# Hybrid RWKV-7 / retention trunk on one core: order of loads, small matrix visits and solves inside the scans, and one visit for four norm sums

## The chip, the cores and the metric

One core of a Trainium2 chip runs the whole program. The metric is the device time of one launch in microseconds (us). PE is the tensor engine, DVE the vector engine, ACT the scalar engine, POOL the GpSimd engine, SP the engine that issues the DMAs. Each of them works through its own instructions in program order; semaphores make one wait for another.

## What is computed

Two layers over 256 latent and 256 context tokens, width 2048. The change lies wholly in the first one, whose core is a delta-rule scan over a 64x64 state of each of 32 heads, in two directions:

```python
def wkv7_scan(S0, r, decay, k, v, kk, a, reverse):
    def step(S, inp):
        r_t, w_t, k_t, v_t, kk_t, a_t = inp
        sa = jnp.einsum('bhvk,bhk->bhv', S, kk_t)
        S = S * w_t[:, :, None, :] - sa[..., None] * (kk_t * a_t)[:, :, None, :] + v_t[..., None] * k_t[:, :, None, :]
        return S, jnp.einsum('bhvk,bhk->bhv', S, r_t)
...
def rwkv7_mixer(h_lat, h_ctx, need_ctx, ...):
    ...
    for d in range(2):
        S_c, oc = wkv7_scan(S0, r_c, w_c[d], k_c[d], v_c, kk_c, a_c[d], d == 1)
        _, ol = wkv7_scan(S_c, r_l, w_l[d], k_l[d], v_l, kk_l, a_l[d], d == 1)
```

Afterwards come a group norm, a gate, the output product with `rk_w_out` (2048x2048), the residual, an RMS norm over the 2048 channels (the four norm sums of the title) and the second layer, which the change leaves alone.

## The kernel before

Each direction is cut into chunks of 64 tokens, eight of them (four of context, then four of latents). The 32 heads stand in pairs: `e` is one of 16 tiles of two heads, and two tiles `E` and `E + 1` are scanned at the same time as two chains. A step `s` (0 to 7) of a chain handles one chunk of both directions. On the engines it is this loop:

- `z` (L1333, PE): the chunk's rows times the state; `zc` (L1338, DVE) adds a part `zv` that needs no state.
- `u` (L1352, PE): multiplies by the inverse of a triangular 64x64 matrix, `tt`; `uc` (L1358, ACT, two instructions) puts it into `uv` with its sign turned.
- `sm` (L1365, PE): the chunk's contribution to the state; `sc` (L1378, or L1380 at s = 0; DVE, four instructions) makes the new state, which the chain's next `z` needs. `qs` (L1343, ACT) scales the old state ahead of it.

Two steps of both chains make a group `q` (0 to 3), so that a pair of tiles has four groups and the scans have 8 x 4 = 32. Each group also has four small visits of PE that work on its matrices and not on the states:

- `first` (L1290): 32 products of 32x32 (fp32 ones count as two instructions in the trace: x32), that need the loaded matrix `it` of both tiles and the small inverse `t1`; `cp1` (L1297, ACT) copies the result.
- `second` (L1303): again 32x32, makes the off-diagonal quarter of the inverse, and `cp2` (L1313, ACT, four copies of 32x128) puts it into `tt`. From then on the group's `u` may run.
- `zv` (L1278): 64x64 products of `it` and `uv`; `zvc` (L1283, ACT) copies it.
- `outs` (L1406, L1414, L1421): the group's outputs, 128x64.

All other PE work in the same stretch is large 128x128x512 matmuls: the tail of the projections (L783) at the beginning, and from L1546 on the output product `rk_w_out`, called out_chunk, whose sums DVE adds into the residual (L1555) once a PSUM bank is complete. DVE also runs `inverse` (L1113, L1120), an elimination of 60 small instructions a pair, and the group norm of finished tiles.

The order on PE, DVE, ACT and POOL is written by hand: `Wheel.at(t, ...)` gives each piece a time on a planned line, `Wheel.run` emits them in the order of these times (a piece waits where a ring of buffers that it names in `need` is full), and chains the instructions so that nothing reorders them. The times are no clock: each engine runs as soon as what it needs is there. Within a group, `h0` is the planned start, `Ts` the planned length of one chain's step (chain `E + 1` stands one `Ts` behind `E`; a chain's own step comes each 2 Ts). The numbers that the change touches are these: `UB = 0.5`, `SB = 1.05` (when `u` and `sm` of a step are due, in Ts), `first` at h0 - 1.1 Ts, `zv` at h0 - 0.7 Ts, `second` at h0 - 0.3 Ts, `outs` at h0 + 4.05 Ts.

SP is not chained by the line: its DMAs are placed by the scheduler, and it issues them in order. Of a group it issues for each of the two tiles `ft` (L1220, 896 KB: `it`, `bt` and a part of `kr` in one; L1221, 128 KB: the rest of `kr`) and two halves of `uv` (L1226, 64 KB each), and for both together `tt` (L1259, eight pieces of 16 KB). There are four `ft` buffers, two of which a group takes, so a group's loads wait for the `outs` of the group two before it.

After the scans four sums of squares a column group (`nrm`, L1574, four column groups `eg`) are put on PE one by one, each into its own 32 rows of one PSUM bank.

## Time and profile before

| | us |
|---|---|
| median of 3 runs | 2784.47 |
| lowest, highest | 2777.64, 2790.91 |
| the profiled execution, its own time | 2789.24 |
| its span, first to last instruction | 2787.4 |
| the scans, from the first `first` to the last `outs` | 1014 to 1680 |
| out_chunk on PE | 1215 to 1729 |
| norm sums (L1574) on PE | 1708 to 1735 |

The span is 1.8 us shorter than the execution's own time. In the profile's rows a group of instructions has its busy time; "idle before" is the time in which its engine had nothing running ahead of it, with the engine or the DMA that ended this. PEld is the weight load of PE, which runs beside its matmuls. PEclk is the granted clock of PE, 1.00 being full speed. In a timeline row stand the start, the length, the engine, the line, the operation, and behind an x how many instructions were merged; since the ends of matmuls are modelled and overlap, the distance between two starts tells more than a length.

### The profile page before, as it was taken

The numbers are of one execution on the slowest core, as the hardware profiler recorded it, in microseconds if no ns is written. First come the engines' busy times: TensorE is split into PE (matmuls) and PEld (weight loads), VectorE is DVE, ScalarE is ACT, GpSimd is POOL, SyncE is SP. The second block draws the span as 40 slices with busy tenths as digits, with TensorE's granted clock in tenths as the row PEclk, the third lists the DMA queues.
The fourth block names the chain that finished last, engine by engine and source line by source line (L and its number), as shares of the span: only waits on it lengthen the run. The fifth ranks groups of instructions, "written<-read, shape, count | busy, mean of one in ns | idle before, by whom it ended". The sixth has DMA issues, their size and how long they took to land. (4 is left out here: it accounts for less than half of the span.)

```text
span 2787.4 us, 48089 instructions
## 1 busy us (share of the span) xinstructions
PE 2653.6 (95%) x18580; PEld 2135.4 (77%) x18580; DVE 1704.2 (61%) x3110; ACT 1317.7 (47%) x2274; POOL 494.5 (18%) x362
## 2 busy tenths in 40 slices
PE   7999999999998999978889999999999999999998
PEld 5576478777776778867777775788888898899886
DVE  3565853678888945677667655965555643434444
ACT  5243742477777524544444443554444533334443
POOL 0002400000004232221222222210000089700000
PEclk9999999999999999998999999999999999999999
DMA  9869873569898776766657565565555666644654
GB/s 340 298 242 313 295 268 121 153 201 275 260 271 254 225 215 191 200 225 198 211 176 213 163 184 196 187 204 187 170 178 175 232 239 218 215 136 152 205 185 162
DMA packets 525686, 594.68 MB, mean 213 GB/s; under 512 B 116993, under 2 KB 358545, under 8 KB 522641
## 3 DMA queue, kind: packets, MB, share of 16 engines
q1 hardware_dynamic: 525458, 591.61, 66.6%
q8 instruction: 146, 2.39, 0.4%
q14 instruction: 82, 0.67, 0.1%
HBM read 464.11 MB, written 127.40 MB: 212 GB/s over the span
## 5 line engine op out<-in xcount | busy, mean ns | idle before, releaser
L397 DVE TENSOR_TENSOR wlo<-wraw,whi 128x1024 fp32r<-128x1024 f32 (+1 forms) x368 | 460.6, 1253 | 570.4 <-ACT whi L396 558.4
L396 ACT CAST whi<-wraw 128x1024 fp32r<-128x1024 f32 (+1 forms) x368 | 375.7, 1024 | 601.9 <-PE ps_acc L423 175.3
L423 PE MATMUL ps_acc<-whi,xop 128*128 128x512 f32 x1024 | 305.0, 392 | 1.3 <-DVE ev L645 0.8
L1919 PE MATMUL ps_acc<-xop,whi 128*128 128x256 f32 (+1 forms) x1024 | 255.8, 343 | 3.6 <-ACT whi L396 2.3
L423 PEld LDWEIGHTS ps_acc<-whi,xop 128*128 128x128 f32 x1024 | 192.1, 188 | 45.3 <-issue 2.9
L1546 PE MATMUL ps_b<-yx,whi 128*128 128x512 f32 x512 | 213.2, 445 | 5.1 <-DVE x L1555 3.6
L1919 PEld LDWEIGHTS ps_acc<-xop,whi 128*128 128x128 f32 x1024 | 178.1, 192 | 27.0 <-ACT whi L396 2.7
L1819 PEld LDWEIGHTS ps_b<-ax,xop 128*128 128x128 f32 x1536 | 190.8, 188 | 4.9 <-DVE ah L397 0.3
L1819 PE MATMUL ps_b<-ax,xop 128*128 128x256 f32 x1536 | 194.4, 282 | 0.1
L423 PE MATMUL ps_acc<-wlo,xop 128*128 128x512 f32 x512 | 187.1, 392 | 0.0
L729 PE MATMUL ps_acc<-xop,whi 128*128 128x512 f32 x512 | 177.9, 407 | 2.0 <-DVE ev L645 2.0
L580 PE MATMUL ps_acc<-xop,whi 128*128 128x512 f32 x512 | 161.7, 402 | 14.3 <-ACT xop L396 12.6
L1919 PE MATMUL ps_acc<-xop,wlo 128*128 128x256 f32 (+1 forms) x512 | 172.3, 338 | 0.0
L1358 ACT ACTIVATE uv<-ps_p 64x128 f32<-64x128 f32 x256 | 69.5, 271 | 212.1 <-PE ps_p L1352 205.8
L1869 PE MATMUL ps_acc<-whi,ah 128*128 128x512 f32 x512 | 161.6, 396 | 1.9 <-DVE ah L397 1.8
L423 PE MATMUL ps_c<-whi,xop 128*128 128x512 f32 x512 | 155.3, 390 | 0.0
L1892 POOL TENSOR_TENSOR wga<-wga,cst 128x512 f32<-128x512 f32 x64 | 71.0, 1129 | 413.1 <-DMA wga<-in_ada_w 412.9
L1537 POOL TENSOR_TENSOR wlo<-wraw,whi 128x512 fp32r<-128x512 f32 (+1 forms) x48 | 80.6, 1679 | 327.2 <-ACT whi L1536 234.4
L580 PEld LDWEIGHTS ps_acc<-xop,whi 128*128 128x128 f32 x512 | 96.1, 191 | 53.6 <-ACT xop L396 16.3
L1378 DVE SCALAR_TENSOR_TENSOR s<-ps_p,ec,qs 64x64 f32<-64x64 f32 x384 | 108.6, 283 | 28.3 <-PE ps_p L1365 21.0
L1546 PEld LDWEIGHTS ps_b<-yx,whi 128*128 128x128 f32 x512 | 97.3, 193 | 29.3 <-issue 10.5
L1113 DVE TENSOR_TENSOR invT<-invX 128x30 f32<-128x30 f32 (+14 forms) x240 | 102.0, 425 | 21.3 <-DMA invX<-Ld 15.7
(299 smaller groups left out, 5609.8 us busy)
## 6 DMA issues: line engine op xcount, KB each, us to landing
wada<-in_ada_w SPq DMA_DIRECT2D x72, 1024.0 KB, 7.8
wraw<-in_rt_w_in SPq DMA_DIRECT2D x64, 1024.0 KB, 5.2
ft<-fD SPq DMA_DIRECT2D x64, 896.0 KB, 6.9
wraw<-in_rk_w_in SPq DMA_DIRECT2D x72, 512.0 KB, 4.8
fD<-it SPq DMA_DIRECT2D x64, 512.0 KB, 4.3
wraw<-in_rt_w_in SPq DMA_DIRECT2D x64, 512.0 KB, 4.8
wraw<-in_rt_w_out SPq DMA_DIRECT2D x32, 1024.0 KB, 5.1
wraw<-in_rk_w_in SPq DMA_DIRECT2D x28, 1024.0 KB, 6.0
```

The lines of the kernel that those rows point to most:

```text
L396: self.nc.scalar.copy(hi, src)
L397: (eng or self.nc.vector).tensor_tensor(lo, src, hi.bitcast(F32), ALU.subtract)
L423: nc.tensor.matmul(pt, xop(d)[:, x_, xs], ws[k // 2][w_][:, k % 2, sl], start=(d == 0 and n == 0), stop=(d == nk - 1 and n == 2))
L580: nc.tensor.matmul(acc[i], (hi, lo)[w_][:, kk, 128 * i:128 * i + 128], xs[ds[k]][:, x_, :], start=(k == 0 and n == 0), stop=(k == nk - 1 a ...
L729: nc.tensor.matmul(st["acc"][i], st["s", d // 4][w_][:, d % 4, 128 * i:128 * i + 128], self.kx[d][:, x_, :], start=(d == 0 and m == 0), st ...
L1113: nc.vector.tensor_tensor(tmp[:, 0:j, 0:n], X[:, 0:j, j].unsqueeze(2).broadcast_to([128, j, n]), X[:, j, j + 1:].unsqueeze(1).broadcast_to ...
L1378: nc.vector.scalar_tensor_tensor(dst, src, ec, R["qs", d][H, H], ALU.mult, ALU.add)
L1537: nc.gpsimd.tensor_tensor(lo[:, 0:n, :], src, hi[:, 0:n, :].bitcast(F32), ALU.subtract)
L1546: nc.tensor.matmul(Q["p", i], Q["s", i // 2][w_][:, k, 128 * (i % 2):128 * (i % 2) + 128], st["yx", e0 + k][:, x_, :], start=(k == 0 and r ...
L1819: nc.tensor.matmul(pt[:, TL * j:TL * j + TL], ht[e][:, w_, 128 * k:128 * k + 128], ax[:, k, x_, :], start=(k == 0 and n == 0), stop=(k == ...
L1869: nc.tensor.matmul(acc[m], y[:, x_, kk, 128 * m:128 * m + 128], ws[w_][:, kk, :], start=(p == 0 and kk == 0 and n == 0), stop=(p == 7 and ...
L1919: nc.tensor.matmul(acc[i][:, 0:nt], w_[:, kk, 128 * i:128 * i + 128], x[:, x_, 0:nt], start=(d == 0 and n == 0), stop=(d == KD - 1 and n = ...
```

## The change

Five things are changed.

1. `ready` of the wheel: a piece may now ask for several buffers of one ring, so one piece `loads(E, q)` can take the `ft` buffers of both tiles.
2. The loads of both tiles are one piece, and each `ft` is loaded in three DMAs: the columns of `it` (512 KB) of both tiles, then the `uv` halves, then the rest (384 KB and 128 KB) of both.
3. `first` and `zv` stand behind each other at h0 - 0.9 Ts; `second` stands at h0 + 0.049 Ts, `outs` at h0 + 4.17 Ts, which is 0.17 Ts into the next group.
4. `u` is due at 0.62 Ts (`UB`) and `sm` at 1.15 Ts (`SB`). The columns of `first` and `second` in PSUM are those of `slot`, so `cp2` takes two copies of 32x256 instead of four of 32x128.
5. The four sums of a column group are put on PE in one piece.

The diff, without the lines that only rename:

```diff
     def ready(self, e):
+        k = {}
         for r, n, _ in e[4]:
             h = self.ring.setdefault(r, [])
-            if len(h) >= n and h[-n] not in self.gone:
+            m = n - k.get(r, 0)
+            if len(h) >= m and h[-m] not in self.gone:
                 return False
+            k[r] = k.get(r, 0) + 1
         return True
...
-UB, SB = 0.5, 1.05
+UB, SB = 0.62, 1.15
...
-            def loads(e, q):
+            def loads(E, q):
...
-                    ft = self.next_ft()
-                    nc.sync.dma_start(ft[:, :, 0:896], self.fD[e, n, :, :, 0:896])
-                    nc.sync.dma_start(ft[:, :, 960:1088], self.fD[e, n, :, :, 896:])
...
-                    w = self.sp.tile([128, 2, 2, 128], F32, name="uv", tag="uv", bufs=FR)
-                    for p in range(2):
-                        r = slice(64 * p, 64 * p + 64)
-                        nc.sync.dma_start(w[r, :, p, :], self.vcD[e, r, n - n % 2:n - n % 2 + 2])
...
+                    ft, w = {}, {}
+                    for e in (E, E + 1):
+                        ft[e] = self.next_ft()
+                        nc.sync.dma_start(ft[e][:, :, 0:512], self.fD[e, n, :, :, 0:512])
+                    for e in (E, E + 1):
+                        w[e] = self.sp.tile([128, 2, 2, 128], F32, name="uv", tag="uv", bufs=FR)
+                        for p in range(2):
+                            r = slice(64 * p, 64 * p + 64)
+                            nc.sync.dma_start(w[e][r, :, p, :], self.vcD[e, r, n - n % 2:n - n % 2 + 2])
+                    for e in (E, E + 1):
+                        nc.sync.dma_start(ft[e][:, :, 512:896], self.fD[e, n, :, :, 512:896])
+                        nc.sync.dma_start(ft[e][:, :, 960:1088], self.fD[e, n, :, :, 896:])
...
-                        hb, o = 64 * (1 - p), 128 * d + 64 * (e % 2) + 32 * h
+                        hb, o = 64 * (1 - p), 64 * slot(e, d, p) + 32 * h
...
-                    for d in range(2):
-                        for p in range(2):
-                            hb = 64 * (1 - p)
-                            r = slice(hb, hb + 32)
-                            x = slot(0, d, p)
-                            nc.scalar.copy(st[E]["tt", q][r, x:x + 3:2, :, hb + 32:hb + 64],
-                                           P["y"][r, 128 * d:128 * d + 128].rearrange("p (m h c) -> p m h c", h=2, c=32))
+                    for p in range(2):
+                        hb = 64 * (1 - p)
+                        r = slice(hb, hb + 32)
+                        nc.scalar.copy(st[E]["tt", q][r, :, :, hb + 32:hb + 64],
+                                       P["y"][r, 0:256].rearrange("p (s h c) -> p s h c", h=2, c=32))
...
-                        if eg == 0 and i == 0:
+                        if eg == 0:
                             self.pn = self.psum("c")
-                        nc.tensor.matmul(self.pn[32 * i:32 * i + 32, :], self.ones, Q["q", i], start=(eg == 0), stop=(eg == 3))
+                        for k in range(4):
+                            nc.tensor.matmul(self.pn[32 * k:32 * k + 32, :], self.ones, Q["q", k], start=(eg == 0), stop=(eg == 3))
...
-                        W.at(te + 4, nrm(i), "fin", (), ((eg, i),))
+                        if i == 3:
+                            W.at(te + 4, nrm(i), "fin", (), tuple((eg, k) for k in range(4)))
...
-                    W.at(h0 - 0.7 * Ts, zv, (j, "z"), (("c", 2, (j, "z")),))
-                    W.at(h0 - 0.7 * Ts + 0.02, zvc, (j, "z"), (), ((j, "z"),))
-                    W.at(h0 - 1.1 * Ts, first, j, (("c", 2, (j, 0)),))
-                    W.at(h0 - 1.1 * Ts + 0.9, cp1, j, (), ((j, 0),))
-                    W.at(h0 - 0.3 * Ts, second, j, (("c", 2, (j, 1)),))
-                    W.at(h0 - 0.3 * Ts + 0.7, cp2, j, (), ((j, 1),))
+                    W.at(h0 - 0.9 * Ts, first, j, (("c", 2, (j, 0)),))
+                    W.at(h0 - 0.9 * Ts + 0.001, zv, (j, "z"), (("c", 2, (j, "z")),))
+                    W.at(h0 - 0.9 * Ts + 0.5, cp1, j, (), ((j, 0),))
+                    W.at(h0 - 0.9 * Ts + 0.52, zvc, (j, "z"), (), ((j, "z"),))
+                    W.at(h0 + 0.049 * Ts, second, j, (("c", 2, (j, 1)),))
+                    W.at(h0 + 0.051 * Ts, cp2, j, (), ((j, 1),))
...
-                    W.at(h0 + 4.05 * Ts, outs(E, q), (E, "o"), tuple((("o", e % 2), 1, ("o", e)) for e in (E, E + 1)) if q == 0 else (),
+                    W.at(h0 + 4.17 * Ts, outs(E, q), (E, "o"), tuple((("o", e % 2), 1, ("o", e)) for e in (E, E + 1)) if q == 0 else (),
```

What this does to the order shows at three places. The first is PE around `first` (L1290) and `zv` (L1278) of one group in the middle of the scans; `ps_b` rows are out_chunk's matmuls, a row without x is one matmul, L1333 is a `z` and L1352 a `u`. Before:

```order
L1290 MATMUL ps_c<-t_13699,ft_8762 32x32 x8
L1290 MATMUL ps_c<-t_13699,ft_8764 32x32 x8
L1546 MATMUL ps_b_13787<-yx,whi 128x512
L1333 MATMUL ps_p_13790<-s_8794,ft_8760 128x128
L1333 MATMUL ps_p_13790<-s_8802,ft_8760 128x128
L1546 MATMUL ps_b_13787<-yx,whi 128x512
L1546 MATMUL ps_b_13787<-yx,wlo 128x512
L1278 MATMUL ps_c<-uv,ft_8762 64x64 x8
L1278 MATMUL ps_c<-uv,ft_8764 64x64 x8
L1546 MATMUL ps_b_13787<-yx,whi 128x512
L1352 MATMUL ps_p_13790<-z,tt_8770 128x64 x2
```

The same place in the changed kernel, where the lines of `z`, `first`, `zv`, out_chunk and `u` are L1339, L1298, L1286, L1552 and L1358:

```order
L1339 MATMUL ps_p_13775<-s_8794,ft_8760 128x128
L1339 MATMUL ps_p_13775<-s_8802,ft_8760 128x128
L1298 MATMUL ps_c<-t_13701,ft_8762 32x32 x8
L1298 MATMUL ps_c<-t_13701,ft_8764 32x32 x8
L1286 MATMUL ps_c<-uv,ft_8762 64x64 x8
L1286 MATMUL ps_c<-uv,ft_8764 64x64 x8
L1552 MATMUL ps_b_13772<-yx,whi 128x512
L1552 MATMUL ps_b_13772<-yx,wlo 128x512
L1552 MATMUL ps_b_13772<-yx,whi 128x512
L1358 MATMUL ps_p_13775<-z,tt_8770 128x64 x2
```

`first` has moved behind the `z` that it preceded, and `zv` follows it with no large matmul between.

The second place is DVE behind a `zc` (L1338) two steps ahead of `first`: L1378 is the new state, L1555 the residual's sum, the others are the elimination. Before:

```order
L1338 TENSOR_TENSOR z<-ps_p_13696,zv 128x128
L1378 SCALAR_TENSOR_TENSOR s_8778<-ps_p_13632,ec,qs 64x64 x2
L1378 SCALAR_TENSOR_TENSOR s_8786<-ps_p_13632,ec,qs 64x64 x2
L1120 TENSOR_TENSOR invX<-invX,invT 128x2x29
L1555 SCALAR_TENSOR_TENSOR x_11073<-ps_b_13556,adac,x_11073 128x256 x2
L1113 TENSOR_TENSOR invT<-invX 128x3x28
```

In the changed kernel the same rows have the lines L1344, L1384, L1123, L1561 and L1116:

```order
L1344 TENSOR_TENSOR z<-ps_p_13698,zv 128x128
L1123 TENSOR_TENSOR invX<-invX,invT 128x2x29
L1561 SCALAR_TENSOR_TENSOR x_11075<-ps_b_13541,adac,x_11075 128x256 x2
L1384 SCALAR_TENSOR_TENSOR s_8778<-ps_p_13613,ec,qs 64x64 x2
L1384 SCALAR_TENSOR_TENSOR s_8786<-ps_p_13613,ec,qs 64x64 x2
L1116 TENSOR_TENSOR invT<-invX 128x3x28
```

An elimination step and two sums of the residual now stand ahead of the state's update. Of the 14 places of a pair of tiles, seven have the sums ahead of the update; at the others at most one small elimination step is ahead.

The third place is SP at the loads of one group (`ft_8766` is the first tile's buffer, `ft_8760` the second's). Before:

```order
L1221 DMA ft_8766<-fD 128x2x128
L1220 DMA ft_8766<-fD 128x2x896
L1226 DMA uv<-vcD 64x2x128 x2
L1220 DMA ft_8760<-fD 128x2x896
L1221 DMA ft_8760<-fD 128x2x128
L1226 DMA uv<-vcD 64x2x128 x2
```

In the changed kernel, with `it` in L1225, `uv` in L1230 and the rest of `ft` in L1232 and L1233:

```order
L1232 DMA ft_8766<-fD 128x2x384
L1225 DMA ft_8766<-fD 128x2x512
L1230 DMA uv<-vcD 64x2x128
L1225 DMA ft_8760<-fD 128x2x512
L1230 DMA uv<-vcD 64x2x128 x3
L1233 DMA ft_8766<-fD 128x2x128
L1232 DMA ft_8760<-fD 128x2x384
L1233 DMA ft_8760<-fD 128x2x128
```

The scheduler still puts a part of the first tile's rest ahead of `it`, but the second tile's `it` now goes out without the 384 KB behind it and as the fourth DMA instead of the fifth.

## The prediction

> **What bounds the kernel now.** I read the page's head first, then the busy time by stage, then PE's waits inside the scans, and last the timelines of PE, SP and DVE around those waits.

> ```profile
> span 2787.4 us, 48089 instructions
> PE 2653.6 (95%) x18580; PEld 2135.4 (77%) x18580; DVE 1704.2 (61%) x3110; ACT 1317.7 (47%) x2274; POOL 494.5 (18%) x362
> ```

> PE is the bound of the whole. The change touches only the scans and the short piece behind them; there the busy times are (columns: length, then PE, PEld, DVE, ACT, POOL, clock, DMA share, GB/s):

> ```profile
> 1014.00:1214.00 200.00, 185.53 (x2026) 154.41 (x2024) 117.44 (x302) 90.42 (x227) 48.55 (x26) 0.97 0.67 194
> 1214.00:1690.00 476.00, 433.06 (x5157) 355.09 (x5157) 323.38 (x902) 210.42 (x594) 116.11 (x82) 0.95 0.63 192
> ```

> PE idles 14.5 + 42.9 = 57 us in the two, and its clock is below full for a few per cent. So a gain must come from PE's waits, from the clock, or from a cheaper visit. The waits from 1010 to 1690:

> ```profile
> PE ps_p L1352 <- DVE z L1338: 22.3, 20, 2.6
> PE ps_c L1290 <- DMA ft<-fD: 20.4, 15, 3.8
> PE ps_p L1333 <- DVE s L1380: 6.2, 1, 6.2
> ```

> `u` waits for DVE (22.3 us, 20 times) and `first` for a load (20.4 us, 15 times). The third wait is one event at the start of a pair, and nothing in the change reaches it.

> **The loads: 18 us.** PE's timeline has two of `first`'s waits and their neighbours:

> ```profile
> 1276.03 0.64 PE L1290 MATMUL ps_c<-t,ft 32*32 32x32 f32 x16 [3.17 <-DMA ft<-fD]
> ...
> 1390.94 0.44 PE L1290 MATMUL ps_c<-t,ft 32*32 32x32 f32 x16 [1.48 <-DMA ft<-fD]
> ...
> 1427.78 0.44 PE L1290 MATMUL ps_c<-t,ft 32*32 32x32 f32 x16
> 1431.98 0.64 PE L1290 MATMUL ps_c<-t,ft 32*32 32x32 f32 x16 [3.76 <-DMA ft<-fD]
> ...
> 1632.79 0.44 PE L1290 MATMUL ps_c<-t,ft 32*32 32x32 f32 x16 [2.14 <-DMA ft<-fD]
> ```

> The wait is in the middle of the visit: its first half runs at 1427.78, its second half needs the second tile's `ft`. SP issued these loads so:

> ```profile
> 1421.67 0.54 SPq L1221 DMA_DIRECT2D ft<-fD  x1
> 1422.31 0.56 SPq L1220 DMA_DIRECT2D ft<-fD  x1
> 1422.96 1.25 SPq L1226 DMA_DIRECT2D uv<-vcD  x2
> 1424.31 0.56 SPq L1220 DMA_DIRECT2D ft<-fD  x1
> ```

> Until `first` could go on, 128 + 896 + 128 + 896 = 2048 KB were issued in 1431.98 - 1421.67 = 10.3 us. By the new order of SP, 384 + 512 + 64 + 512 = 1472 KB stand there in four DMAs instead of five. The relief is at least one issue, 1422.96 - 1422.31 = 0.65 us, and one `z` that now stands ahead of `first` (0.45 us, below): 1.1 us. It is at most the bytes' share, 576/2048 x 10.3 = 2.9, plus 0.45: 3.35 us. I take the middle, 2.2 us. It ends all waits but the two longest, which keep 0.97 and 1.56: 20.4 - 2.5 = **18 us** (12 with 1.1 us taken from each of the 15, as far as they reach; 20 with 3.35). The `outs` that free the buffers move 0.12 Ts later, `first` 0.2 Ts later; that difference is the `z` already counted. The later `rest` has cover until `outs` and the state's product, both behind `first`; SP's 64 further issues, some 0.6 us each, are off the path.

> **The clock: 10 us.** Behind these waits the granted clock is half. The first two rows are two of the seven stretches in which this is seen, then their sum; the last two, of another answer, are the same work of a group, from `z` to `outs`, slow and fast:

> ```profile
> 1392.10:1395.40 3.30, 3.30 (x34) 2.65 (x34) 2.29 (x8) 0.75 (x2) 0.00 (x0) 0.50 0.36 130
> 1429.60:1436.40 6.80, 4.42 (x49) 3.61 (x51) 2.07 (x7) 0.73 (x2) 0.00 (x0) 0.50 0.65 205
> sum 37.05, PE 34.08 PEld 27.98 DVE 16.96 ACT 8.47 POOL 3.29; mean PE 4.87 PEld 4.00 DVE 2.42 ACT 1.21 POOL 0.47
> ...
> 1276.60:1287.11 10.51, 10.51 (x129) 8.64 (x125) 4.83 (x11) 3.98 (x11) 2.42 (x2) 0.54 0.15 25
> 1355.51:1361.80 6.29, 6.29 (x127) 5.18 (x125) 4.11 (x12) 4.26 (x11) 1.57 (x1) 1.00 0.35 111
> ```

> At half clock 1 - 6.29/10.51 = 0.40 of the time is lost: 34.08 x 0.40 = 13.6 us if all seven go. Several lie close to a wait of `u` too, which may stay, so I take **10 us**. The lower end is 6 us, if only the stretches behind 3.17 and 3.76 us go (about 10.1 and 4.4 us of PE).

> [...]

> **One visit for `first` and `zv`: 5 us.** No row shows both together; what a visit's edges cost is seen at `second`:

> ```profile
> 1437.38 0.48 PE L1546 MATMUL ps_b<-yx,whi 128*128 128x512 f32 x1
> 1437.80 0.69 PE L1303 MATMUL ps_c<-tt,x 32*32 32x32 f32 x32
> 1438.42 0.50 PE L1546 MATMUL ps_b<-yx,wlo 128*128 128x512 f32 x1
> 1438.75 0.40 PE L1546 MATMUL ps_b<-yx,whi 128*128 128x512 f32 x1
> ```

> A large matmul takes 0.22 us from start to start (below). Into the visit it is 0.42, out of it 0.33: the two changes of shape cost 0.20 + 0.11 = 0.31. The merge leaves three changes of four (in, 32x32 to 64x64, out). It saves 0.31 x 32 groups = 10 us if the middle change is free, nothing if it costs as much as two, 0.16 x 32 = **5 us** if it costs like the others, which I take. By order, `second` and `outs` don't come to stand together.

> [...]

> **Norm sums: 2 us.** A single sum and a run of sums:

> ```profile
> 1707.34 0.39 PE L1546 MATMUL ps_b<-yx,whi 128*128 128x512 f32 x1
> 1707.66 1.04 PE L1574 MATMUL ps_c<-sq,ones 128*32 128x512 f32 x2
> 1708.63 0.50 PE L1546 MATMUL ps_b<-yx,whi 128*128 128x512 f32 x1
> ...
> 1729.41 2.81 PE L1574 MATMUL ps_c<-sq,ones 128*32 128x512 f32 x16
> ```

> Alone it costs 0.97 + (0.32 - 0.22) = 1.07 us; in a run 2.81/8 = 0.35. Only the first column group's four are separate before. Then 4 x 1.07 becomes 1.07 + 3 x 0.35, so 4.3 - 2.1 = **2 us** (0 if the last sum's input is late, 3 if the fixed part vanishes).

> **Later solves, and the state behind other work: -4 us.** DVE's timeline and PE's at the same place:

> ```profile
> 1382.92 0.29 DVE L1338 TENSOR_TENSOR z<-ps_p,zv 128x128 f32<-128x128 f32 x1
> 1383.12 1.19 DVE L1378 SCALAR_TENSOR_TENSOR s<-ps_p,ec,qs 64x64 f32<-64x64 f32 x4
> 1384.34 0.39 DVE L1113 TENSOR_TENSOR invT<-invX 128x220 f32<-128x220 f32 x1
> 1384.76 0.88 DVE L1555 SCALAR_TENSOR_TENSOR x<-ps_b,adac,x 128x256 f32<-128x256 f32 x2
> ...
> 1387.14 0.28 DVE L1338 TENSOR_TENSOR z<-ps_p,zv 128x128 f32<-128x128 f32 x1
> ```

> ```profile
> 1384.35 0.39 PE L1546 MATMUL ps_b<-yx,whi 128*128 128x512 f32 x1
> 1384.57 0.61 PE L1333 MATMUL ps_p<-s,ft 128*128 128x128 f32 x4
> 1385.02 0.61 PE L1365 MATMUL ps_p<-uv,ft 128*128 128x128 f32 x4
> ...
> 1387.48 0.66 PE L1352 MATMUL ps_p<-z,tt 128*128 128x64 f32 x4 [1.16 <-DVE z L1338]
> ```

> (1384.57 - 1384.35 and 1385.02 - 1384.57 are the 0.22 and 0.45 used above.) DVE has a queue of 1387.14 - 1382.92 = 4.2 us from one `zc` to the next, so `u` waits 1.16 us. The state is done at 1384.31, and `z` takes it at 1384.57: a slack of 0.26 us. In the changed order L1555 (0.88 us) stands ahead of the state's update at seven of 14 places, so `z` would wait 0.88 - 0.26 = 0.62 us there, with the chain's `sm` and all of out_chunk behind it on PE. The scans take 666/8 = 83 us a pair, and out_chunk runs beside 465 us of them, 5.6 pairs: 39 places, 24 us. A wait at `z` delays the `u` behind it, whose wait shrinks as much: 20 x 0.62 = 12 us come back, which leaves a loss of 12. On the other side, `u` stands 0.12 x 83/16 = 0.62 us later on the line; if all 20 waits shrank by this without a new one, 12 us would be gained. In the tight steps the order has no more large matmuls between `z` and `u` than before, so I take a value on the side of the loss, **-4 us**.

> **`cp2`: nothing.** Four ACT copies become two of twice the width:

> ```profile
> L1313 ACT COPY tt<-ps_c x128: 254/256/258, 1019.7 to 1660.6; 32x128 f32<-32x128 f32 x128
> ```

> That is between 2 x 0.256 less and no change for each group, on an engine busy 47%, with `s`, `outs` and large matmuls between `second` and the `u` that needs it. `second` itself now stands 0.35 Ts later; without that cover `u` would wait for the copies, 32 x 0.5 = 16 us at most. The new `ready` changes no time: one `outs` frees both buffers.

> **The sum** is 18 + 10 + 5 + 2 - 4 = 31 us. On the profiled execution, 2789.24, this gives 2758; that execution lies 4.8 us above the median of the runs, from which the same sum gives 2753. I say **2755**.

> **Rivals.**
> - *The loads gain only half* (0.15). SP still issues 384 KB of the first tile ahead of its `it`, and the scheduler may do worse elsewhere. For it: 1472 of 2048 KB is no large cut. Then 9 + 5 + 5 + 2 - 4 = 17 us: about 2770.
> - *DVE takes over* (0.20). The 4.2 us queue between two `zc` isn't shortened by a new order, and PE's waits for `ft` are time in which DVE catches up. Then the 18 us come back as waits of `u` and `z`, with half of the clock's gain: 31 - 18 - 5 = 8, about 2779. Against it: DVE is busy 323 of 476 us.
> - *Slower* (0.08). The update of the state stands behind L1555 and an elimination step (0.39 us), so `z` waits 1.0 us at 39 places, 39 us, and no `u` wait goes. If each third wait is followed by a half-clock stretch of 3.4 us, that is 13 x 3.4 x 0.40 = 18 us more. Against this stand 18 + 5 + 2 = 25: about 2789 + 32 = 2821, or 2816 from the median. It decides once PE idles more than some 0.65 us ahead of `z` at each such place (39 x 0.65 = 25).

> **How the numbers follow.** The forecast has 0.57. Its own ends are 20 + 14 + 10 + 3 + 12 = 59 and 12 + 6 + 0 + 0 - 12 = 6 us, so 2728 to 2781 between the two bases; the range takes in the DVE case up to 2785. A measurement of this kernel tells about 0.5% from no change, 14 us, so faster means below 2770.5: most of the forecast (0.49), over half of the first rival (0.09) and a part of the second (0.07), 0.65. Slower is the last rival, 0.08; the rest is 0.27.

> **What would show it.** Right: `first`'s wait for `ft` (L1298) falls from 20.4 to about 2 us; the half-clock stretches behind it are gone; `zv` (L1286) starts about 0.6 us behind `first` with no matmul of L1552 between; one `nrm` visit of some 2 us; the last `outs` about 28 us earlier. Wrong: waits of `z` (L1339) for the state (L1384), or of `u` (L1358), that sum to over 40 us, with a new half-clock stretch behind them.

## The result, and the profile after

| | before | changed |
|---|---|---|
| median, us | 2783.70 of 4 runs | 2757.09 of 4 runs |
| lowest, highest | 2777.64, 2790.91 | 2754.68, 2763.23 |
| profiled execution, its span | 2789.24, 2787.4 | 2757.53, 2755.8 |

The ratio is 0.9893 (0.9867 to 0.9920): 26.6 us less by the medians, where 29.5 was forecast and 2755 as the time. The total came out. The terms behind it did not all, and most of what follows is about that.

The head of the page after:

```profile
span 2755.8 us, 48109 instructions
PE 2634.0 (96%) x18572; PEld 2129.6 (77%) x18580; DVE 1717.6 (62%) x3110; ACT 1309.9 (48%) x2210; POOL 493.4 (18%) x362
```

For the stages one needs borders that mean the same in both kernels. The first `first` doesn't, since the change moves it. I take the last of the projections' small matmuls ahead of the scans (L1021, in the changed kernel L1024) and the last `outs`. The windows between them, before and then after (length; PE, PEld, DVE, ACT and POOL busy; clock; DMA share; GB/s):

```profile
984.20:1680.10 695.90, 634.89 (x7229) 525.86 (x7229) 442.21 (x1206) 302.75 (x820) 177.20 (x135) 0.96 0.65 195
```

```profile
984.00:1653.20 669.20, 620.63 (x7222) 521.09 (x7230) 451.05 (x1206) 294.80 (x757) 177.26 (x135) 0.97 0.71 203
```

The scans are 26.7 us shorter. PE's idle time went from 695.9 - 634.9 = 61.0 to 48.6 us, 12.4 less, and its busy time fell by 14.3 at the same work: that is clock and cheaper visits. Summed from the granted clock, 61.4 us of the stage before stood at half clock, in 13 stretches, and 37.5 after, in five; PE was busy for 54.4 us of the former and 26.0 us of the latter. The stretch from the last `outs` to the second layer's first product went from 60.6 to 56.7 us. All else agrees within 1.5 us.

PE's waits from 1010 to 1690, after (L1339 is `z`, L1358 `u`, L1298 `first`, L1286 `zv`; L1384 and L1386 are the state's update, L1305 is `cp1`):

```profile
PE ps_p L1339 <- DVE s L1386: 13.3, 4, 11.9
PE ps_p L1358 <- DVE z L1344: 11.9, 12, 4.5
PE ps_p L1339 <- DVE s L1384: 7.5, 14, 1.2
PE ps_c L1298 <- DMA ft<-fD: 3.2, 3, 1.9
PE ps_c L1286 <- ACT x L1305: 2.5, 3, 0.8
```

Against before: the wait for `ft` is gone but for 3.2 of 20.4 us, `u` waits 11.9 instead of 22.3, and `z` waits for the state 7.5 us at 14 places where it did not before. The first row is the surprise. Before, it was one wait of 6.2 us; now it is one of 11.9 and three short ones, 1.4 us in all. The next rows show where it comes from, on PE, DVE and SP:

```profile
1189.98 0.56 PE L1358 MATMUL ps_p<-zv,tt 128*128 128x64 f32 x4
1202.42 1.19 PE L1339 MATMUL ps_p<-s,ft 128*128 128x128 f32 x4 [11.88 <-DVE s L1386]
```

```profile
1188.54 0.39 DVE L1116 TENSOR_TENSOR invT<-invX 128x220 f32<-128x220 f32 x1
1199.89 0.09 DVE L1189 MEMSET ones<- 128x32 f32 x1 [10.96 <-DMA gT<-ge]
```

```profile
1187.08 0.52 SPq L1233 DMA_DIRECT2D ft<-fD  x1
1187.70 1.37 SPq L1225 DMA_DIRECT2D ft<-fD  x1
...
1192.46 1.25 SPq L1232 DMA_DIRECT2D ft<-fD  x2
1193.76 0.61 SPq L1233 DMA_DIRECT2D ft<-fD  x1
1194.46 0.55 SPq L796 DMA_DIRECT2D gT<-ge  x1
```

In `open_scans2` DVE sets a tile `ones` to 1.0, and this memset waits for a DMA that carries the last gate tile `ge` to DRAM. What can tie the two together is memory: the new pool seems to lie where the DMA's source is released. SP issues that DMA behind the loads of a whole group, 2048 KB of `ft` and the `uv` halves. Before, it stood between the two tiles' loads:

```profile
1201.69 0.54 SPq L793 DMA_DIRECT2D gT<-ge  x1
1202.33 0.54 SPq L1220 DMA_DIRECT2D ft<-fD  x1
```

So the new piece of loads, which takes both tiles at once, has pushed one transfer back that has nothing to do with it, and DVE, then PE, wait 5.7 us longer for it. A window over the stretch behind it is at half clock for its full length:

```profile
1194.50:1214.80 20.30, 11.37 (x96) 10.03 (x97) 12.38 (x27) 6.23 (x16) 5.48 (x4) 0.50 0.61 205
```

These 20.3 us are more than half of the 37.5 us at half clock that the scans have left. They are neither all new nor all lost. At the same place the kernel before has 10.2 us at half clock (between 1204.3 and 1218.0, PE busy for 6.3 of them), and in the first 8 of the 20.3 us PE stands idle. Its busy time there is 11.4 us, so by the 0.40 of the prediction the longer stretch costs an estimated 2 us (5.1 x 0.40) beside the wait.

### The profile page after: what moved, and what is told of

Its sections match the earlier page's. It is cut to its first block, busy times and chain, and to the rows that moved or that the text cites. A ratio compares the mean times of both kernels' runs of the same rounds, so it can differ in the third digit from the quotient of the medians.

```text
span 2755.8 us, 48109 instructions
## 1 busy us (share of the span) xinstructions
PE 2634.0 (96%) x18572; PEld 2129.6 (77%) x18580; DVE 1717.6 (62%) x3110; ACT 1309.9 (48%) x2210; POOL 493.4 (18%) x362
## 5 line engine op out<-in xcount | busy, mean ns | idle before, releaser
L1552 PE MATMUL ps_b<-yx,whi 128*128 128x512 f32 x512 | 203.4, 434 | 1.0 <-DVE x L1561 1.0
L583 PE MATMUL ps_acc<-xop,whi 128*128 128x512 f32 x512 | 162.3, 403 | 13.6 <-ACT xop L399 13.0
L1384 DVE SCALAR_TENSOR_TENSOR s<-ps_p,ec,qs 64x64 f32<-64x64 f32 x384 | 108.4, 282 | 61.3 <-PE ps_p L1371 55.6
L1116 DVE TENSOR_TENSOR invT<-invX 128x30 f32<-128x30 f32 (+14 forms) x240 | 121.3, 505 | 22.2 <-DMA invX<-Ld 17.3
L426 PEld LDWEIGHTS ps_acc<-wlo,xop 128*128 128x128 f32 x512 | 96.7, 189 | 20.9 <-issue 0.5
```

The lines of the kernel that those rows point to most:

```text
L426: nc.tensor.matmul(pt, xop(d)[:, x_, xs], ws[k // 2][w_][:, k % 2, sl], start=(d == 0 and n == 0), stop=(d == nk - 1 and n == 2))
L583: nc.tensor.matmul(acc[i], (hi, lo)[w_][:, kk, 128 * i:128 * i + 128], xs[ds[k]][:, x_, :], start=(k == 0 and n == 0), stop=(k == nk - 1 a ...
L1116: nc.vector.tensor_tensor(tmp[:, 0:j, 0:n], X[:, 0:j, j].unsqueeze(2).broadcast_to([128, j, n]), X[:, j, j + 1:].unsqueeze(1).broadcast_to ...
L1384: nc.vector.scalar_tensor_tensor(dst, src, ec, R["qs", d][H, H], ALU.mult, ALU.add)
L1552: nc.tensor.matmul(Q["p", i], Q["s", i // 2][w_][:, k, 128 * (i % 2):128 * (i % 2) + 128], st["yx", e0 + k][:, x_, :], start=(k == 0 and r ...
```

## The experiments

All times are medians, with the ratio to the kernel before from the same chip and its 95% interval. "Scans" is the stage between the two borders above, "half" the time in it at half clock; these and the waits, all in us, come from the one profiled execution of each kernel, which can lie some us off the median (visits 5.6 above it, UB with SB 8.0). "Half, all" is the time at half clock in the whole launch, averaged over all executions of a kernel (60 of the kernel before): 2 x (1 - mean granted clock) x span, since the clock in the traces of the kernel before and of the changed one is 0.5 or 1.00 and nothing between. These averages are good to some 3 or 4 us. The prediction's 0.40 us per us was worked out for PE at work; among the 60 executions before, one with 10 us less of half clock is 4.9 us shorter on the average, so 0.40 is not too high a price for them either. "gT" is `z`'s waits for the state of s = 0: the one behind that memset, in the changed kernel with three others of 1.4 us, and with the old loads in it three of 2.2 us. "z" is its waits for the other states.

| kernel | us | ratio | scans | half | half, all | `ft` | `u` | z | gT |
|---|---|---|---|---|---|---|---|---|---|
| before | 2783.7 | 1 | 695.9 | 61.4 | 114 | 20.4 | 22.3 | 0 | 6.2 |
| + loads | 2769.8 | 0.9952 (0.9935 to 0.9969) | 681.7 | 47.8 | 95 | 9.5 | 25.9 | 0 | 11.6 |
| + visits | 2769.2 | 0.9952 (0.9933 to 0.9970) | 684.5 | 54.6 | 93 | 11.5 | 24.4 | 0 | 6.9 |
| + UB, SB | 2769.5 | 0.9942 (0.9923 to 0.9961) | 683.3 | 51.2 | 95 | 16.9 | 10.5 | 5.4 | 7.6 |
| + norm sums | 2783.1 | 0.9993 (0.9976 to 1.0010) | 694.6 | 64.9 | 119 | 21.1 | 22.0 | 0 | 6.7 |
| changed | 2757.1 | 0.9893 (0.9867 to 0.9920) | 669.2 | 37.5 | 90 | 3.2 | 11.9 | 7.5 | 13.3 |
| changed, old loads | 2765.5 | 0.9936 (0.9913 to 0.9959) | 679.1 | 44.4 | 101 | 13.8 | 9.2 | 7.8 | 9.4 |
| changed, old visits | 2755.1 | 0.9904 (0.9880 to 0.9929) | 670.4 | 41.0 | 84 | 5.8 | 15.1 | 4.5 | 12.2 |
| changed, old UB, SB | 2761.5 | 0.9919 (0.9899 to 0.9940) | 677.4 | 34.1 | 86 | 5.2 | 25.2 | 0 | 11.8 |

### One part at a time, added to the kernel before

The loads (with `ready`, which they need):

```diff
...
-                    for e in (E, E + 1):
-                        W.at((h0 - LD + 1.7 * (e - E) if E or q else tl + 1.5 + e - E), loads(e, q), "fl", (("f", FR, (e, q)),))
+                    W.at(h0 - LD if E or q else tl + 1.5, loads(E, q), "fl", tuple(("f", FR, (e, q)) for e in (E, E + 1)))
```

> The kernel before with the new loads alone (and the ready that they need). Theory L (the loads are the main term, as predicted): first's wait for ft falls from 20.4 us to under 6, most of the half-clock stretches behind it go, and the time falls by 15 to 28 us, to about 2760. Theory P (the place of first does it, one z later): the wait stays over 12 us and the time falls by under 10 us. Theory D (DVE takes over): the wait for ft goes, but PE's wait for z of L1338 rises from 22 us to over 32, and the time falls by under 10 us.

The time is 13 us shorter by the ratio and 16 by the medians, at the lower end of theory L; the wait for `ft` halves and doesn't go, so theory L is right only in part. Against theory D, `u`'s wait rises by 3.6 us only. Not in any theory was the third row:

```profile
PE ps_p L1360 <- DVE z L1346: 25.9, 21, 2.9
PE ps_p L1341 <- DVE s L1388: 11.6, 1, 11.6
PE ps_c L1298 <- DMA ft<-fD: 9.5, 6, 2.4
```

The wait behind the memset goes from 6.2 to 11.6 us with the loads alone, and it is 6.2 to 7.6 in every kernel with the old loads. (In the changed kernel with the old loads four waits sum to 9.4, the longest 7.2.) So it is the loads' doing.

The visits (`first` and `zv` at h0 - 0.9 Ts, `second` at h0 + 0.049 Ts, `outs` at h0 + 4.17 Ts, two copies in `cp2`):

> The kernel before with the four small visits at their new places (first and zv, second and outs) and the two copies of cp2, with the old loads and solves. Theory L: 5 us from the merged visit and some 6 us of the wait for ft, so 5 to 12 us faster, with 12 to 16 us of that wait left. Theory P: the wait for ft falls below 8 us and the time by 15 us or more.

More than theory L said and less than theory P: 13 to 16 us, with 11.5 us of the wait for `ft` left. The new places relieve this wait about as much as the new loads do. That it is the place of `first`, behind a `z`, is argued and not shown, since this run moves four visits at once.

UB and SB, then each of the two alone:

```diff
-UB, SB = 0.5, 1.05
+UB, SB = 0.62, 1.15
```

> The kernel before with UB and SB of the changed kernel alone. Theory L (as predicted, the later solves cost 4 us): the wait of u for z falls by 5 to 12 us, new waits of z for the state come up with as much or more, the time is from 2 us faster to 8 us slower. Rival S (the later solves are a gain of their own): u's waits fall from 22 to about 12 us with few waits of z, and the time falls by 8 us or more.

> The kernel before with UB = 0.62 alone (SB stays 1.05): u stands later, the state's update stays where it was. If u's place brings the gain of the two numbers (14 to 16 us together): u's wait for z falls from 22 to about 11 us, no wait of z for the state, 10 us or more faster. If SB brings it: within 5 us of before, u's wait at 18 us or more.

> The kernel before with SB = 1.15 alone (UB stays 0.5): the state's product and update stand later on PE and DVE. By the prediction (the update behind the residual's sums makes z wait): about 5 us of waits of z for the state, u's wait falls by as much or less, time from 2 us faster to 8 us slower. If SB brings the gain of the two: u's wait falls by 8 us or more, 10 us or more faster.

Rival S is right in the time, 14 to 16 us faster, and in `u`'s waits; `z` does wait for the state, 5.4 us at 11 places. The waits with both, then with UB alone, then with SB alone:

```profile
PE ps_p L1352 <- DVE z L1338: 10.5, 13, 1.5
PE ps_p L1333 <- DVE s L1380: 7.6, 1, 7.6
PE ps_p L1333 <- DVE s L1378: 5.4, 11, 0.9
```

```profile
PE ps_p L1352 <- DVE z L1338: 14.9, 17, 2.1
```

```profile
PE ps_p L1352 <- DVE z L1338: 16.5, 18, 1.7
PE ps_c L1290 <- DMA ft<-fD: 14.2, 6, 4.5
PE ps_p L1333 <- DVE s L1380: 8.6, 6, 6.5
PE ps_p L1333 <- DVE s L1378: 5.0, 10, 0.9
```

Neither of my two alternatives holds for the single numbers: each gives about half, 0.9970 (0.9951 to 0.9988) for UB and 0.9967 (0.9953 to 0.9980) for SB. UB's place takes 7.4 us of `u`'s wait away, with 0.2 us of new waits of `z`. SB's part is not explained by these waits: `u` waits 5.8 us less, but `z` waits 7.4 more (5.0 behind L1378, and 8.6 instead of 6.2 behind L1380). The single profiled executions can't say more, since the one with UB alone lies 8 us above its own median, with 81.9 us of half clock in the scans. The clock of all executions can. On this chip the kernel before has 116 us of half clock in a launch, with UB alone it is 106, with SB alone 95. Times the 0.40 of the prediction the difference is an estimated 4 of UB's 8 us and 8 of SB's 8. So SB gains by the clock, and UB by the clock and the waits; why a later update of the state keeps the clock up is not shown by any run.

The norm sums:

```diff
-    W.at(te + 4, nrm(i), "fin", (), ((eg, i),))
+    if i == 3:
+        W.at(te + 4, nrm(i), "fin", (), tuple((eg, k) for k in range(4)))
```

> The kernel before with the four norm sums of a column group in one piece alone. As predicted: 2 us faster (0 to 3), from the first column group's four visits of 1.07 us that become one of about 2.1 us. Rival: 4 to 5 us, since from the last out_chunk to the second layer's first product the changed kernel's trace is shorter by more than that.

The time can't tell this from nothing. The trace can: from the last `outs` to the second layer's first product it is 56.8 us instead of 60.6, 3.8 less, and 56.7 in the changed kernel. All six traces with single sums have 58.8 to 60.8 us there, all eight with four in one 55.4 to 56.8. In the changed kernel the visit reads:

```profile
1683.90 0.40 PE L1552 MATMUL ps_b<-yx,whi 128*128 128x512 f32 x1
1684.23 1.06 PE L1581 MATMUL ps_c<-sq,ones 128*32 128x512 f32 x8
1685.22 0.50 PE L1552 MATMUL ps_b<-yx,whi 128*128 128x512 f32 x1
```

Four sums take 0.99 us from start to start, where a single one took 0.97.

### One part at a time, taken out of the changed kernel

> The changed kernel with the loads of before. If the pieces add up (the loads alone gave 13 to 16 us): 2769 to 2773, with first's wait for ft at over 10 us. If they overlap: 2757 to 2763; the wait for gT, 11.9 us in the changed kernel and 6 to 8 in every kernel with the old loads, would be shorter by 4 us and pay for a part of it.

> The changed kernel with the four visits (and cp2) of before at their old places. If the pieces add up (the visits alone gave 13 to 16 us): 2769 to 2773, with first's wait for ft at over 8 us. If they overlap: 2757 to 2763, with that wait at 4 to 8 us.

> The changed kernel with UB and SB of before. If the pieces add up (UB and SB alone gave 14 to 16 us): 2769 to 2773, u's wait back at over 20 us, z's wait for the state (7.5 us) gone. If the pieces overlap (each takes away the same half-clock stretches and the same stalls): within 6 us of the changed kernel, 2757 to 2763.

The parts overlap. Added alone, loads, visits and UB with SB gave 0.48 + 0.48 + 0.58 = 1.5%, by the medians 48 us; together, with the norm sums, they gave 1.1%, 26.6 us. Taken out again, the loads cost 8.4 us by the medians (between overlap and addition), UB and SB 4.5 (as overlap says), and without the new visits the kernel is no slower: 2755.1, 2 us under what overlap says, the intervals one on the other. Two causes are in the table. Loads and visits work on the same 20.4 us: 10.9 and 8.9 us less alone, 15.2 together (without UB and SB). And each of the three alone takes 19 to 21 us of half clock off the launch, but all together only 24: by the 0.40 of the prediction, some 14 of the missing 21 us.

### The wait behind the memset

First the memset alone was moved, to where it is needed:

```diff
-        self.nc.vector.memset(self.ones, 1.0)
...
+            W.at(te[KD] - 20, lambda: nc.vector.memset(self.ones, 1.0))
```

> The changed kernel with the memset of ones (DVE, needed only by the norm sums) moved from the opening of the second stage of the scans to 20 units of the line before its end. In the changed kernel DVE stands 11.0 us at this memset for the DMA gT<-ge, whose source lies where ones goes, and PE 11.9 us for the state behind it. Theory W (the wait is the memset's alone): the 11.9 us go and a part of the 20 us of half clock around them, so 10 to 20 us faster than the changed kernel, about 2737 to 2747. Rival: another transfer or the DVE queue is due at the same time, a wait of over 6 us stays at this place, and the time is within 5 us of the changed kernel's.

2750.68 us, 0.9884 (0.9855 to 0.9912): 6.4 us better by the medians, 2.5 by the ratios, less than theory W. The 11.9 us are gone, and a 7.6 us wait of ACT for the same DMA has come: the first write of `whi` needs it too, so its pool seems to lie over `ge` as well. PE then waits 4.9 us for what stands behind it on ACT:

```profile
1198.36 0.62 ACT L1541 CAST whi<-wraw 128x512 fp32r<-128x512 f32 x1 [7.62 <-DMA gT<-ge]
```

```profile
1199.55 0.80 PE L1551 MATMUL ps_b<-yx,whi 128*128 128x512 f32 x1 [4.92 <-ACT yx L1522]
```

So the rival had a part of it: not another transfer, but another reader of the same one. Then the cause itself, the order on SP, for this one group, the tenth of the 32 (the expectations call it the sixth; `self.lastg` is the DMA gT<-ge, and `after_g` is called on the loads of `ft` of this group):

```diff
...
+            def after_g(i):
+                tc.add_manual_dep(i, self.lastg, mybir.DependencyInfo(
+                    mybir.DependencyClass.NoSync, mybir.DependencyReason.DATA), reason="line")
...
-                    W.at(h0 - LD if E or q else tl + 1.5, loads(E, q), "fl", tuple(("f", FR, (e, q)) for e in (E, E + 1)))
+                    W.at((max(h0 - LD, tx - 0.01) if (E, q) == (4, 1) else h0 - LD) if E or q else tl + 1.5, loads(E, q), "fl", tuple(("f", FR, (e, q)) for e in (E, E + 1)))
```

> The changed kernel in which the loads of one group (the sixth of the scans) are issued behind the last DMA gT<-ge and no longer ahead of it. Moving the memset alone gave 5 to 7 us and left a wait of ACT for the same DMA (7.6 us), with 4.9 us of PE behind it. Theory G (the new loads cost time only by standing ahead of this DMA on SP): the 11.9 us wait of z falls to under 3, ACT's wait for gT goes too, and the kernel is 12 to 22 us faster than the changed one, about 2735 to 2745. Rival: what comes behind (the residual's and out_chunk's first loads, the group's own loads now later) takes the place: a wait of 5 us or more for ft or wraw at the same place, and under 7 us gained.

2747.40 us, 0.9872 (0.9854 to 0.9890), 9.7 us better than the changed kernel by the medians and 6 by the ratios, whose intervals overlap. The scans of its trace are 661.5 us long, 7.7 less. SP issues the DMA at 1184.53, ahead of the loads, and `z` waits 3.4 us in place of 11.9:

```profile
1184.53 0.54 SPq L796 DMA_DIRECT2D gT<-ge  x1
1185.12 1.20 SPq L1230 DMA_DIRECT2D ft<-fD  x2
```

```profile
1189.63 1.19 PE L1350 MATMUL ps_p<-s,ft 128*128 128x128 f32 x4 [3.38 <-DVE s L1397]
```

The loads of the group, now later, cost nothing: the wait for `ft` is 3.4 us in all. So the mechanism of theory G is right, and the gain is below its 12 to 22 us because the clock gave little. The half clock in the scans is 27.3 us, 10 less, but what went is mostly time in which PE stood idle: its busy time at half clock is 24.0 us, 2.0 less. And `u`'s waits behind this place stay, 7.1 us where the changed kernel has 7.5.

Both edits together:

> The changed kernel with both: the sixth group's loads behind the last DMA gT<-ge, and the memset of ones late. The first alone gave 10 us and left 3.4 us of z waiting for the state behind that memset. If the two add (the memset's wait goes, ACT's wait for gT stays short): 1 to 5 us faster than with the order alone, 2742 to 2746. If ACT's whi now waits for the DMA in its place: within 2 us, 2746 to 2750.

2745.19 us, 0.9870 (0.9853 to 0.9886). `z` still waits 1.6 us for the state there. This is the fastest kernel of the study by its median, 11.9 us below the changed one (6 by the ratios, since the kernel before is 3 us faster on this chip too); against the order on SP alone the difference of 2.2 us is not told by the intervals.

## Why the prediction was right, and where it wasn't

**The loads, 18 us.** The mechanism and its size were right: the wait for `ft` fell from 20.4 to 3.2 us, 17.2. But it was put down to the loads alone, with the `z` ahead of `first` a small part. The loads alone take 10.9, the visits alone 8.9. The step that failed is the sentence that SP's further issues are off the path: it looked at how many DMAs are issued and not at which foreign DMA stands behind them. That one transfer costs 5.7 us more of PE's wait, and moving it back gave 6 to 10.

**The clock, 10 us.** PE's busy time at half clock in the scans fell from 54.4 to 26.0 us, and 28.4 times the 0.40 of the prediction is 11. All executions agree, with 24 us less of half clock in a launch. So the size is right. The account behind it is right only in part: it has seven stretches, 37 us, behind the waits for `ft`, but the scans before have 13, 61.4 us, and of the other six four lie behind waits of `u` or of `z` for the state. The loads are not the only ones to relieve them: alone, they take 19 us of half clock off the launch, the visits 21, and UB with SB 19. What stands ahead of such stretches differs: the one from 1194.4 on in the changed kernel begins 3.8 us into the wait of 11.9, and the one at 1392.04 in the kernel before stands behind a wait of 1.48 us. How long PE was busy ahead of each stands in the last section.

**One visit for `first` and `zv`, 5 us.** The changed kernel's timeline, where the clock was full:

```profile
1446.65 0.69 PE L1298 MATMUL ps_c<-t,ft 32*32 32x32 f32 x32
1447.27 1.15 PE L1286 MATMUL ps_c<-uv,ft 64*64 64x64 f32 x32
1448.35 0.50 PE L1552 MATMUL ps_b<-yx,whi 128*128 128x512 f32 x1
```

`first` takes 0.62 us to the start of `zv`, as `second` did to the start of a large matmul, and `zv` 1.08, its median with large matmuls on both sides before. So the change from 32x32 to 64x64 cost here what the one from 32x32 to a large matmul did, 0.62 us to the next start, and what goes is the one entry from a large matmul into `zv` (0.33 instead of 0.23): 0.10 x 32 = 3 us. The step was right, and its size a little high. These 3 us come from rows alone; in no run's time do they stand by themselves, and the changed kernel without the new visits is no slower.

**Norm sums, 2 us.** 3.2 from the rows: four visits of 1.07 became one of 0.99 + (0.33 - 0.23) = 1.09. The term took 0.35 us for each further sum; here three cost 0.02 us (0.99 - 0.97). It was the upper bound that held.

**UB and SB, -4 us.** Here the sign was wrong. The step that failed is that `z` would wait 0.62 us at each of 39 places. The count of the places is right: in the trace after, 39 updates of the state stand behind the residual's sums. The price is near too, 7.5 us at 14 places, 0.54 each. But `z` waits behind 12 of the 39 only: the slack of 0.26 us, read at one place, was taken for all. `u`'s wait, meanwhile, fell by 10.4, not far from the 12 that the prediction set against the loss. And the term has nothing for the clock, which by all executions gives an estimated 8 us (114 to 95 us of half clock, times 0.40) of the 14 to 16 that the two numbers bring alone. I chose the loss between two ends of equal size because large matmuls between `z` and `u` had not become more in the tight steps I had looked at; the kernel with UB alone loses a third of `u`'s waits for 0.2 us of new ones.

**What was not in the sum.** New waits of `zv` for `cp1` (2.5 us), and the 5.7 us behind gT. The terms that were found make up what the two traces differ by in the scans, 26.7 us: of the 12.4 us of idle time, 17.2 + 10.4 less for `ft` and `u`, 7.5 + 7.1 + 2.5 more for the state and `cp1`, and small ones; of the 14.3 busy, the clock's 11 and the visits' 3. With UB and SB undervalued and the side effect of the loads missed, two errors of opposite sign made the total come out so near: that part was luck. As forecast, the copies of `cp2` show nowhere: PE has no wait for them among those from 1010 to 1690.

**The rivals.** DVE did not take over: `u` and `z` together wait 11.9 + 7.5 = 19.4 us for the chain through DVE, 22.3 before (with the states of s = 0, where the DMA is what DVE waits for, 32.7 and 28.5). The loads that gain half did occur in the kernel with the loads alone, whose wait for `ft` fell by 10.9 of 20.4 us. The slower case was far: 14 waits with a mean of 0.54 us where it needed 39 over 0.65.

## What to carry to other kernels

When loads are put in a better order, read the queue for what stands behind them that belongs to nobody in the change: here a store whose source's memory the next pool seems to take over, and a memset of 0.09 us that held PE for 12. An order of instructions tells where a wait can arise, not that it does; count such places by the slack that the trace shows at each. And parts that work on the same wait are not to be summed: three that gave 1.5% one by one gave 1.1% together. Where one execution's waits don't explain a gain, as with SB, the clock of all executions may.

## What the runs showed of the hardware

Four norm sums in a row, 128x32 each into another quarter of the PSUM rows, took 0.99 us from start to start; one alone took 0.97 us.
